# The start of an encoder layer on one core: dummy matmuls ahead of the data, and another cut and order of the first loads

## The chip, the cores and the metric

The kernel runs on one core of one Trainium2 chip. The metric is the device time of one execution in microseconds; the kernel before has a median of 1192.68 us over 3 runs (1192.55 to 1193.81). Engines are named as in the profile: PE is the matrix engine and PEld its weight loads, DVE the vector engine, ACT the scalar engine, POOL GpSimd, SP the engine that issues nearly all DMAs here.

## The reference

One encoder layer over 1024 tokens of width 1024, all in float32, cut to what matters here:

```python
hn = rms_norm(x, norm1_g)
proj = hn @ w_in                      # 2304 columns: qA | kA | vA | qB | kB | vB
out_a = global_gqa_attention(rope(norm(qa)), rope(norm(ka)), va)
out_b = dilated_mixture_attention(norm(qb), norm(kb), vb)
x = x + concat(rms_norm(out_a), rms_norm(out_b)) @ w_out
x = x + conv_ffn(rms_norm(x, norm2_g), w_up, conv_w, conv_b, w_down)
```

The change is confined to the loads and the first matmuls of `hn @ w_in`. The gain `norm1_g` is multiplied into the weights' rows, and the division by the root mean square of a token follows later, so the first matmuls need only `x`, `w_in` and `norm1_g`.

## The kernel before, in words

**Numbers.** A float32 operand is split into a high part, rounded by ACT (`split` L245, first line), and a low part, the difference, from DVE (L247). A product takes three matmuls: high by high, high by low, low by high. So every operand costs one ACT and one DVE instruction before PE can use all of it, and the first matmul of three needs ACT's half alone.

**Two kinds of work on PE at the start.** The 256 columns of kA and vA are projected plainly: for each of 8 token tiles, `kv_proj` (L294) does 8 contraction steps of 3 matmuls of 128x256, 24 in all, on L299, L300 and L301. Their weights `w_kv` are split by `kv_split` (L286), which also multiplies by the gain, and x by `x_prep` (L256), one split for each half (512 of the 1024 contraction rows) of a tile. The other 2048 columns are projected by a seven-product block scheme in two chunks; `in_unit` (L431) is one contraction step of one product over four token tiles, 12 matmuls of 128x512 on L437 to L439, with weights that `w_prep` (L402) makes from the blocks "11", "12", "21", "22" of `w_in`. The first product (4 units, 48 matmuls) takes x and block "11" alone; the second, n = 5, takes block "12" too, and sums of x halves (`x_sum` L262, `s_split` L279).

**Where x lies.** A tile's two halves are stored 4 tiles apart in one buffer: half h of tile tt at `qab((tt + 4h) % 8) + 512h` (L249). `x_load_t` (L252) loads both with one strided DMA of 512 KB.

**What sets the order.** A scheduler orders each engine's instructions within what the code's order and the buffers allow, and puts semaphore waits before them; engines then run their lists strictly in order. SP's DMAs take eight semaphores in turn (DMAHW0 to DMAHW7), so a DMA waits until the one eight before it on the list has landed. The start is L579 to L602: the two halves of `w_kv`, tile 0 of x, the gain vector (`norm1_g`, 32 bytes a partition), the other tiles 1 to 3, block "11", the splits, then the identity matrix, four small loads that spread the head gains over the partitions, x tiles 4 to 7, block "12", and the rows of x for the mean square (`n_load` L273, one buffer, read by `n_sq` L276 on ACT before the next load). `kv_tile` (L1186) does one tile: `kv_proj`, the `x_prep` of the tile two ahead, and `kv_out` (L309), in which ACT copies the tile's sums out of their PSUM bank (one of four) to a staging buffer at `F_UA + 256 * i`, whence a DMA stores them. `late_consts` (L616) and `bound` (L604) work on the head gains; `bound` uses scratch at `F_UA`, in the staging buffer of tile 0.

The whole program is emitted twice (`emit(True)`, `emit(False)`): the second copy runs only if the head gains are very large, which they are not here. After the first 250 or so matmuls the order of the instructions is not touched by the change.

Of the kernel before, what the change touches and what calls it, by code (L numbers as in the profile page):

```python
# [20 lines left out]
D = 1024  # L21
# [13 lines left out]
O_IDF = 0  # L35
O_GA = 128
O_GB = 384
# [19 lines left out]
SM_G1 = O_SM + 24  # L57
# [8 lines left out]
F_UA = O_F  # L66
F_W = [O_F + 2048 + 2048 * i for i in range(3)]
F_TMP = O_QAB + 512
F_KSQ = O_QAB + 768
F_NG = O_F + 9216  # L70
F_ROPE = O_F + 8192


# [60 lines left out]
C_12 = [O_QAB + 2048, O_QAB + 2560, O_F + 1536, O_F + 8704]  # L134

@with_exitstack
def tile_encoder_layer(ctx, tc, x, xT, w_in, w_kv, gains, norm1_g, norm2_g, w_out, w_up, convs,
                       w_down, ident, rope, tmx, tbc, cnt, tee, out):
    nc = tc.nc
    pool = ctx.enter_context(tc.tile_pool(name="arena", bufs=1))  # L140
    pspool = ctx.enter_context(tc.tile_pool(name="psum", bufs=1, space=bass.MemoryType.PSUM))
# [10 lines left out]
    def emit(bounded):  # L152

        act = nc.scalar.activation
        vec = nc.vector
        gp = nc.gpsimd
        mm = nc.tensor.matmul
        dma = nc.sync.dma_start

        def f(off, n):  # L160
            return bigf[:, off:off + n]

        def r(off, n):
# [33 lines left out]
        def perm_rows(t, b, width):  # L197
            rr, c = divmod(b, 2)
            return bass.AP(tensor=t.tensor, offset=t.offset + (512 * c + rr) * width, ap=[[4 * width, 128], [1, width]])

        def bcast(t, n, off=0):
            return bass.AP(tensor=t.tensor, offset=t.offset + off, ap=[[0, 128], [1, n]])
# [21 lines left out]
        def qab(tt):  # L224
            return O_QAB + 1024 * tt
# [16 lines left out]
        def a_op(n, t):  # L242
            return R_A[n] + 1024 * t

        def split(o, src):  # L245
            act(r(o, 512), src, AF.Copy)
            vec.tensor_tensor(r(o + 512, 512), src, rf(o, 512), op=OP.subtract)  # L247

        def x_at(tt, half):  # L249
            return qab((tt + 4 * half) % 8) + 512 * half  # L250

        def x_load_t(tt):  # L252
            a, b = [x_at(tt, half) for half in ((0, 1), (1, 0))[tt // 4]]
            dma(fp(a, [b - a, 2], [1, 512]), heads(xT[:, tt, :], 2))

        def x_prep(tt):  # L256
            for half in range(2):
                split(a_op(((1, 2), (3, 4))[tt // 4][half], tt % 4), f(x_at(tt, half), 512))

        x_raw = {5: lambda t: x_at(t + 4, 1), 7: lambda t: x_at(t + 4, 0), 6: lambda t: x_at(t, 0), 3: lambda t: x_at(t, 1)}  # L260
# [12 lines left out]
        def n_load(tt):  # L273
            dma(f(F_ROPE, 1024), perm_rows(x, tt, D))

        def n_sq(tt):  # L276
            act(f(F_ROPE, 1024), f(F_ROPE, 1024), AF.Square, accum_out=f(SM_SS1 + tt, 1))

# [1 line left out]
            split(a_op(n, t), f(x_raw[n](t), 512))  # L280


        def kv_load(half):
            dma(f(F_W[2] + 1024 * half, 1024), w_kv[half])

        def kv_split(k):  # L286
            o, raw, g = R_A[7] + 2048 * (k // 4) + 256 * (k % 4), f(F_W[2] + 256 * k, 256), f(SM_G1 + k, 1)
            act(r(o, 256), raw, AF.Copy, scale=g)
            vec.scalar_tensor_tensor(r(o + 1024, 256), raw, g, rf(o, 256), op0=OP.mult, op1=OP.subtract)
# [24 lines left out]
        def k4(o, j, n=64, off=0):  # L314
            return fp(o + 128 * j + off, [1024, 4], [64, 2], [1, n])
# [19 lines left out]
        def k_turn():  # L335
            for j in range(2):
                for o in (0, 16, 32, 48):
                    gp.tensor_tensor(k4(F_KSQ, j, 16, o), k4(F_TMP, j, 16, o ^ 16),
                                     fp(F_ROPE + 512 * j + 64 + o, [128, 4], [0, 2], [1, 16]), op=OP.mult)

        def k_add():
            for j in range(2):
                k = k4(F_TMP, j)
                vec.tensor_tensor(k, k, fp(F_ROPE + 512 * j, [128, 4], [0, 2], [1, 64]), op=OP.mult)
                vec.tensor_tensor(k, k, k4(F_KSQ, j), op=OP.add)
# [56 lines left out]
        def w_prep(m):  # L402
# [6 lines left out]
            if n == 5:  # L409
                act(b12, b12, AF.Copy, scale=g0)  # L410
                vec.scalar_tensor_tensor(b11, b11, f(F_NG + k, 1), b12, op0=OP.mult, op1=OP.add)
            if n == (6 if c else 3):
# [66 lines left out]
        def done(kind, t0, u, late=None):  # L479
# [5 lines left out]
            if kind == "kb":  # L485
                qo, qs = (O_QAB, 1024) if t0 else (F_ROPE, 256)
            elif late is not None:
# [88 lines left out]

            return square_at, mean_at, root_at, refine_at, norm_at, gain_at

        kv_load(0)  # L579
        x_load_t(0)  # L580
        dma(f(SM_G1, 8), norm1_g)
        kv_load(1)
        for i in range(1, 4):
            x_load_t(i)
        w_load(0, "11", 0, 2)
        w_load(0, "11", 2, 2)
        x_prep(0)
        for k in range(8):
            kv_split(k)
        x_prep(1)  # L590
        dma(f(O_IDF, 128), ident)
        for i, o in enumerate((O_GA, O_GA + 128, O_GB, O_GB + 64)):
            dma(f(o, 64), bcast(gains, 64, 64 * i))
        for i in range(4, 6):
            x_load_t(i)
        for i in range(6, 8):
            x_load_t(i)
        w_load(0, "12")
        n_load(0)
        w_load(0, "21", 0, 3)  # L600
        vec.tensor_copy(r(R_IDR, 128), f(O_IDF, 128))
        vec.tensor_scalar(f(F_NG, 8), f(SM_G1, 8), -1.0, None, op0=OP.mult)  # L602

        def bound():  # L604

            t = F_UA
            vec.tensor_tensor(fp(t, [64, 2], [1, 64]), fp(O_GA, [128, 2], [1, 64]), fp(O_GA, [128, 2], [1, 64]), op=OP.mult)
            vec.tensor_tensor(f(t + 128, 64), f(O_GB, 64), f(O_GB + 64, 64), op=OP.mult)
            vec.tensor_tensor(f(t + 128, 64), f(t + 128, 64), f(t + 128, 64), op=OP.mult)
            vec.tensor_reduce(f(t + 192, 3), heads(f(t, 192), 3), axis=AX.X, op=OP.max)  # L610
            vec.tensor_tensor(f(t + 192, 1), f(t + 192, 1), f(t + 193, 1), op=OP.mult)
            vec.tensor_tensor(f(t + 192, 1), f(t + 192, 1), f(t + 194, 1), op=OP.max)
            vec.tensor_scalar(f(O_LIM, 1), f(t + 192, 1), float(HD), None, op0=OP.mult)
            vec.tensor_scalar(f(O_LIM + 1, 1), f(O_LIM, 1), LIMIT, None, op0=OP.is_le)
# [639 lines left out]
        for m in range(4 * len(prods)):  # L1254
            c, n = prods[m // 4]
# [65 lines left out]
        for g in range(16):  # L1321
# [28 lines left out]
            if g > 3 and fills:  # L1350
                b, kv = grp(g - 2 if bounded else g - 1)
# [441 lines left out]
        for m in range(2, len(order)):  # L1793
            j, n = order[m]
# [10 lines left out]
            if n == 3 and j < NPAIR - 1:  # L1805
# [4 lines left out]
                b = [lambda j=j, t=t: taps(j, 0, (t,)) for t in range(1, 5)]  # L1810
# [17 lines left out]
        for m in range(len(steps)):  # L1828
            n, q = steps[m]
# [97 lines left out]
```

## Time and profile before

| | |
|---|---|
| median of 3 runs | 1192.68 us |
| the profiled execution | 1192.58 us |
| its span (first to last instruction) | 1190.8 us, so 1.8 us lie around it |
| PE busy | 1170.1 us, 98% |
| DVE, ACT busy | 1010.8 us (85%), 661.2 us (56%) |
| granted TensorE clock, mean | 0.999 |

Busy time of PE, 98%, includes the time in which its matmuls ran at half pace: the profile counts an instruction as busy as long as it takes. A row of the timeline has the start in us from the span's start, the duration, the engine, the source line, what is written and read, and in brackets how long the engine sat idle before and what ended that. Matmuls overlap: the distance between two starts is what one costs, the duration is longer.

### The profile page before, as it was taken

Reading aid. Unit: us, or ns where it says so; the run is one execution under the profiler, and the core shown is the slowest. Engines: PE = TensorE matmul, PEld = TensorE weight load, DVE = VectorE, ACT = ScalarE, POOL = GpSimd, SP = SyncE. Lnnn points to the kernel's source line nnn. Section 1 sums busy time; section 2 is a strip of 40 time slices with the busy share of each in tenths; the row PEclk is TensorE's granted clock in tenths of the full one; section 3 lists DMA queues with packets and bytes.
Section 4 is the critical chain, followed back from the end, with each engine's and each line's share of the span. In section 5 each row is a group of like instructions: output and inputs, shape, how many; then the busy total and the mean of one; then the engine's idle time right before and its main releaser. Section 6 shows DMA issues by size and latency. Waiting matters only on the chain.

```text
span 1190.8 us, 16352 instructions
## 1 busy us (share of the span) xinstructions
PE 1170.1 (98%) x5876; PEld 963.7 (81%) x5876; DVE 1010.8 (85%) x1430; ACT 661.2 (56%) x986; POOL 332.0 (28%) x236
## 2 busy tenths in 40 slices
PE   6999999999999999999999999999999999999998
PEld 5888887666679998887888888888888888888886
DVE  6887888899988788568999999999999997966663
ACT  6874747789897777336544353444435363543331
POOL 0000221510024420011456565655556414000000
PEclk9999999999999999999999999999999999999999
DMA  8555220020016555222223233332323257967862
GB/s 306 169 168 147 80 69 18 17 61 1 10 40 155 120 129 198 86 72 97 81 80 115 91 114 104 109 107 98 115 80 115 107 203 275 339 226 254 290 222 85
DMA packets 123286, 153.23 MB, mean 129 GB/s; under 512 B 51648, under 2 KB 79040, under 8 KB 123072
## 3 DMA queue, kind: packets, MB, share of 16 engines
q1 hardware_dynamic: 121056, 146.37, 38.1%
q0 software_dynamic: 2144, 5.77, 2.2%
q8 instruction: 47, 0.77, 0.3%
q14 instruction: 39, 0.32, 0.1%
HBM read 113.57 MB, written 33.82 MB: 124 GB/s over the span
## 4 chain that ended last, share of the span: by engine, by line
PE 88%; DVE 5%; DMA 2%; ACT 2%; POOL 1%; issue 1%; SPq 0%; ACTq 0%; DVEq 0%; POOLq 0%
PE ps L1562 12%; PE ps L1561 12%; PE ps L1560 12%; PE ps L740 6%; PE ps L1704 6%; PE ps L1702 6%; PE ps L1703 6%; PE ps L439 3%; PE ps L437 3%; PE ps L438 3%; PE ps L969 3%; PE ps L1004 2%; PE ps L1109 2%; PE ps L1111 2%; PE ps L1110 2%; PE ps L756 2%
## 5 line engine op out<-in xcount | busy, mean ns | idle before, releaser
L1560 PE MATMUL ps<-bigr 128*128 128x512 f32 x616 | 239.8, 390 | 0.5 <-ACT bigr L1163 0.5
L1561 PE MATMUL ps<-bigr 128*128 128x512 f32 x616 | 239.6, 389 | 0.0
L1562 PE MATMUL ps<-bigr 128*128 128x512 f32 x616 | 239.6, 389 | 0.0
L1599 DVE SCALAR_TENSOR_TENSOR bigf<-bigf 128x768 f32<-128x768 f32 (+1 forms) x176 | 193.4, 1135 | 0.7
L1528 ACT ACTIVATE bigr<-bigf 128x512 fp32r<-128x512 f32 x154 | 91.7, 622 | 141.6 <-POOL bigf L1520 109.0
L1682 ACT ACTIVATE bigr<-bigf 128x1024 fp32r<-128x1024 f32 (+1 forms) x99 | 83.9, 868 | 115.8 <-PE ps L1704 83.4
L1560 PEld LDWEIGHTS ps<-bigr 128*128 128x128 f32 x616 | 115.7, 188 | 25.0 <-ACT bigr L1163 0.9
L1562 PEld LDWEIGHTS ps<-bigr 128*128 128x128 f32 x616 | 115.7, 188 | 24.0
L1561 PEld LDWEIGHTS ps<-bigr 128*128 128x128 f32 x616 | 115.7, 188 | 23.8
L1683 DVE TENSOR_TENSOR bigr<-bigf,bigr 128x1024 fp32r<-128x1024 f32 (+1 forms) x99 | 97.5, 1007 | 26.4 <-ACT bigr L1682 21.6
L1702 PE MATMUL ps<-bigr 128*128 128x512 f32 x308 | 119.8, 389 | 0.0
L1703 PE MATMUL ps<-bigr 128*128 128x512 f32 x308 | 119.8, 389 | 0.0
L1704 PE MATMUL ps<-bigr 128*128 128x512 f32 x308 | 119.8, 389 | 0.0
L1529 DVE TENSOR_TENSOR bigr<-bigf,bigr 128x512 fp32r<-128x512 f32 x112 | 106.1, 950 | 3.0 <-ACT bigr L1528 2.6
L740 PE MATMUL ps<-bigr 128*66 128x512 f32 x384 | 99.8, 394 | 0.0
L437 PE MATMUL ps<-bigr 128*128 128x512 f32 x224 | 87.4, 390 | 0.0
L438 PE MATMUL ps<-bigr 128*128 128x512 f32 x224 | 87.2, 389 | 0.0
L439 PE MATMUL ps<-bigr 128*128 128x512 f32 x224 | 87.1, 389 | 0.0
L767 DVE TENSOR_TENSOR bigr<-bigf,bigr 128x1024 fp32r<-128x1024 f32 x64 | 81.0, 1271 | 5.3 <-ACT bigr L766 4.8
L1565 DVE TENSOR_TENSOR bigf<-ps,bigf 128x512 f32<-128x512 f32 x110 | 75.1, 682 | 5.1 <-PE ps L1562 4.8
L1529 POOL TENSOR_TENSOR bigr<-bigf,bigr 128x512 fp32r<-128x512 f32 x42 | 67.0, 1594 | 32.9 <-ACT bigr L1528 31.9
L740 PEld LDWEIGHTS ps<-bigr 128*66 128x66 f32 x384 | 50.9, 136 | 29.8
(220 smaller groups left out, 2380.8 us busy)
## 6 DMA issues: line engine op xcount, KB each, us to landing
bigf<-w_down SPq DMA_DIRECT2D x99, 256.0 KB, 4.0
bigf<-w_up SPq DMA_DIRECT2D x44, 512.0 KB, 3.5
bigf<-gscr SPq DMA_DIRECT2D x77, 256.0 KB, 4.1
gscr<-bigf SPq DMA_DIRECT2D x31, 512.0 KB, 2.7
bigf<-x SPq DMA_DIRECT2D x16, 512.0 KB, 4.4
bigf<-w_in SPq DMA_DIRECT2D x29, 256.0 KB, 3.1
bigf<-xT SPq DMA_DIRECT2D x8, 512.0 KB, 5.1
bigf<-w_out SPq DMA_DIRECT2D x8, 512.0 KB, 3.5
```

Source lines behind the costliest of these rows:

```text
L437: mm(o, r(a, 128), r(w, 512), start=(k == 0 and n != 2 and (c == 1 or n != 3)), stop=False, skip_group_check=True)
L438: mm(o, r(a, 128), r(w + 512, 512), start=False, stop=False, skip_group_check=True)
L439: mm(o, r(a + 512, 128), r(w, 512), start=False, stop=(k == 3), skip_group_check=True)
L740: mm(bank(ob)[0:66], r(w, 66), r(p + 512 * u, 512), start=(kt == 0 and i == 0), stop=(kt == 7 and i == 2))
L1529: low = lambda eng: eng.tensor_tensor(rp(o + 512, [128, 4], [1, 128]), src, rfp(o, [128, 4], [1, 128]), op=OP.subtract)
L1560: mm(bank(b), wh, th, start=(k == 0 and n in (1, 5, 6, 7)), stop=False, skip_group_check=True)
L1561: mm(bank(b), wh, tl, start=False, stop=False, skip_group_check=True)
L1562: mm(bank(b), wl, th, start=False, stop=(k == 3), skip_group_check=True)
L1599: vec.scalar_tensor_tensor(f(a + o, n), f(i + d, n), w_, f(a + o, n), op0=OP.mult, op1=OP.add)
L1702: mm(o, ah, r(d, 512), start=(q == 0 and n in (1, 5, 2)), stop=False, skip_group_check=True)
L1703: mm(o, ah, r(d + 1024, 512), start=False, stop=False, skip_group_check=True)
L1704: mm(o, al, r(d, 512), start=False, stop=(q == NQ - 1), skip_group_check=True)
```

## The change

- Ten matmuls of 128x128 on a buffer filled with ones (by POOL) stand ahead of everything on PE; their result in bank 7 is not used. The buffer is the one that `n_load` fills later.
- `norm1_g` is no array of its own any more: it stands in the 8 columns ahead of the `w_kv` weights, comes with the first quarter of them, and DVE copies it to its old place.
- `w_kv` comes in three DMAs (steps 0-1 with the gains, 2-3, 4-7), with the halves of x tile 0 in between as DMAs of their own; x tile 0's second split stands behind the first four weight splits.
- Every x tile is loaded by two DMAs of 256 KB, one for each half, and the array is laid out on the host so that no half has to be swapped. All eight tiles are issued ahead of the constants and block "12".
- The identity and the head gains, already spread over 128 partitions, are one array of 2 KB a partition with one DMA in place of five.
- `bound`'s scratch moves to `F_UA + 1024`, out of the staging buffer of the first four tiles.

```diff
+WARM = 10
         def x_load_t(tt):
-            a, b = [x_at(tt, half) for half in ((0, 1), (1, 0))[tt // 4]]
-            dma(fp(a, [b - a, 2], [1, 512]), heads(xT[:, tt, :], 2))
-
-        def x_prep(tt):
             for half in range(2):
+                dma(f(x_at(tt, half), 512), xT[:, tt, 512 * half:512 * half + 512])
+
+        def x_prep(tt, halves=(0, 1)):
+            for half in halves:
                 split(a_op(((1, 2), (3, 4))[tt // 4][half], tt % 4), f(x_at(tt, half), 512))
...
-        def kv_load(half):
-            dma(f(F_W[2] + 1024 * half, 1024), w_kv[half])
+        def kv_load(k, n):
+            o = 8 if k == 0 else 0
+            dma(f(F_W[2] + 256 * k - o, 256 * n + o), w_kv[:, 256 * k + 8 - o:256 * (k + n) + 8])
...
-        kv_load(0)
-        x_load_t(0)
-        dma(f(SM_G1, 8), norm1_g)
-        kv_load(1)
+        warm = f(F_ROPE, 256)
+        gp.memset(warm, 1.0)
+        for i in range(WARM):
+            mm(bank(7, 128), f(F_ROPE, 128), f(F_ROPE + 128, 128), start=True, stop=True)
+        kv_load(0, 2)
+        dma(f(x_at(0, 0), 512), xT[:, 0, 0:512])
+        kv_load(2, 2)
+        dma(f(x_at(0, 1), 512), xT[:, 0, 512:1024])
+        kv_load(4, 4)
         for i in range(1, 4):
             x_load_t(i)
         w_load(0, "11", 0, 2)
         w_load(0, "11", 2, 2)
-        x_prep(0)
-        for k in range(8):
+        vec.tensor_copy(f(SM_G1, 8), f(F_W[2] - 8, 8))
+        x_prep(0, (0,))
+        for k in range(4):
+            kv_split(k)
+        x_prep(0, (1,))
+        for k in range(4, 8):
             kv_split(k)
         x_prep(1)
-        dma(f(O_IDF, 128), ident)
-        for i, o in enumerate((O_GA, O_GA + 128, O_GB, O_GB + 64)):
-            dma(f(o, 64), bcast(gains, 64, 64 * i))
-        for i in range(4, 6):
+        for i in range(4, 8):
             x_load_t(i)
-        for i in range(6, 8):
-            x_load_t(i)
+        dma(f(O_IDF, 512), consts)
         w_load(0, "12")
         n_load(0)
...
-            t = F_UA
+            t = F_UA + 1024
```

The lists of SP differ from the first entry on. SP before, from the load of x tiles 1 to 3 on; w_in 128x1024 is half of block "11", 128x2048 is block "12", and a wait on DMAHWn is one for a landing:

```order
L254 DMA bigf<-xT 128x2x512 x3
L397 DMA bigf<-w_in 128x1024
L397 DMA bigf<-w_in 128x1024 [waits DMAHW0_49]
L591 DMA bigf<-ident 128x128 [waits DMAHW1_49]
L593 DMA bigf<-gains 128x64 [waits DMAHW2_49]
L593 DMA bigf<-gains 128x64 [waits DMAHW3_49]
L593 DMA bigf<-gains 128x64 [waits DMAHW4_49]
L593 DMA bigf<-gains 128x64 [waits DMAHW5_49]
L254 DMA bigf<-xT 128x2x512 [waits DMAHW6_49,DVE_49]
L397 DMA bigf<-w_in 128x2048 [waits DMAHW7_49]
L254 DMA bigf<-xT 128x2x512 [waits DMAHW6_49,DMAHW0_49]
L274 DMA bigf<-x 128x1024 [waits DMAHW1_49]
```

SP with the change, from block "11" on:

```order
L399 DMA bigf<-w_in 128x1024 [waits DMAHW3_49]
L399 DMA bigf<-w_in 128x1024 [waits DMAHW4_49]
L255 DMA bigf<-xT 128x512 [waits DMAHW5_49]
L255 DMA bigf<-xT 128x512 [waits DMAHW6_49]
L255 DMA bigf<-xT 128x512 [waits DMAHW7_49]
L255 DMA bigf<-xT 128x512 [waits DMAHW0_49]
L255 DMA bigf<-xT 128x512 [waits DMAHW1_49]
L255 DMA bigf<-xT 128x512 [waits DMAHW2_49]
L255 DMA bigf<-xT 128x512 [waits DMAHW3_49]
L255 DMA bigf<-xT 128x512 [waits DMAHW4_49]
L604 DMA bigf<-consts 128x512 [waits DMAHW5_49]
L399 DMA bigf<-w_in 128x2048 [waits DMAHW6_49,DVE_49]
```

Before, x tile 4 waits for DVE, and x tile 5 waits for tile 4's landing (DMAHW6) beside its own semaphore (DMAHW0); tiles 6 and 7 come further down, each behind the landing of the one before. With the change each half waits for nothing but its turn of the eight semaphores, and all of x stands ahead of the constants and block "12".

ACT's list begins differently. Before (L246 splits x tile 0, L288 splits `w_kv`):

```order
L246 ACT_TABLE_LOAD
L246 ACTIVATE bigr<-bigf 128x512 [waits DMAHW1_49]
L246 ACTIVATE bigr<-bigf 128x512
L288 ACTIVATE bigr<-bigf 128x256 [waits DMAHW2_49,DMAHW0_49]
L288 ACTIVATE bigr<-bigf 128x256 x3
L288 ACTIVATE bigr<-bigf 128x256 [waits DMAHW3_49]
```

With the change (L290 is `kv_split`, L247 the split of x):

```order
L290 ACT_TABLE_LOAD [waits DMAHW0_49]
L290 ACTIVATE bigr<-bigf 128x256 [waits DVE_49]
L247 ACTIVATE bigr<-bigf 128x512 [waits DMAHW1_49]
L290 ACTIVATE bigr<-bigf 128x256
L290 ACTIVATE bigr<-bigf 128x256 [waits DMAHW2_49]
L290 ACTIVATE bigr<-bigf 128x256
L247 ACTIVATE bigr<-bigf 128x512 [waits DMAHW3_49]
L290 ACTIVATE bigr<-bigf 128x256 [waits DMAHW4_49]
```

The load of ACT's function table stood ahead of every wait; now it stands behind the wait for the first quarter of `w_kv`.

Some 50 instructions further, ACT copies the last `kv_proj` tiles out of PSUM (L311 before, L313 with the change); L246 and L247 are splits of x sums, L277 and L278 are `n_sq`, and L413 and L415 scale quarters of block "22". Before:

```order
L311 ACTIVATE bigf<-ps 128x256 [waits DMAHW5_49,PE_49,Activation_49]
L246 ACTIVATE bigr<-bigf 128x512 [waits DVE_49]
L246 ACTIVATE bigr<-bigf 128x512 [waits PE_49]
L413 ACTIVATE bigf<-bigf 128x512 [waits DMAHW7_49]
L246 ACTIVATE bigr<-bigf 128x512 [waits DVE_49]
L311 ACTIVATE bigf<-ps 128x256 [waits DMAHW6_49,PE_49,Activation_49]
L277 ACTIVATE bigf<-bigf 128x1024 [waits DMAHW0_49]
```

With the change:

```order
L278 ACTIVATE bigf<-bigf 128x1024 [waits DMAHW0_49]
L313 ACTIVATE bigf<-ps 128x256 [waits DMAHW7_49,PE_49,Activation_49]
L247 ACTIVATE bigr<-bigf 128x512 [waits DVE_49] x2
L415 ACTIVATE bigf<-bigf 128x512 [waits DMAHW2_49]
L415 ACTIVATE bigf<-bigf 128x512 [waits DMAHW3_49]
L313 ACTIVATE bigf<-ps 128x256 [waits DMAHW1_49,PE_49,Activation_49]
```

Before, one quarter of block "22" stood between the last two copies out of PSUM; now two do, each with a landing to wait for.

More of the change, by code (lines that the diff above doesn't have):

```diff
@@ L136, in tile_encoder_layer @@
 @with_exitstack
-def tile_encoder_layer(ctx, tc, x, xT, w_in, w_kv, gains, norm1_g, norm2_g, w_out, w_up, convs,
-                       w_down, ident, rope, tmx, tbc, cnt, tee, out):
+def tile_encoder_layer(ctx, tc, x, xT, w_in, w_kv, consts, norm2_g, w_out, w_up, convs,
+                       w_down, rope, tmx, tbc, cnt, tee, out):
     nc = tc.nc
@@ L1907 @@
     arrays = {
-        "x": x, "xT": a(np.stack([np.roll(_lanes(x[r].T, D)[0], 512 * (t // 4), axis=-1) for t, r in enumerate(rows)], axis=1)),
+        "x": x, "xT": a(np.stack([_lanes(x[r].T, D)[0] for r in rows], axis=1)),
         "w_in": a(np.stack([np.stack([_lanes(w_in[:, at:at + 512], 512)[half] for half in range(2) for _, at in c])
                             for c in CHUNKS])),
-        "w_kv": a(_lanes(w_in[:, 512:768], 512)),
-        "gains": np.concatenate([a(qa_norm_g), a(ka_norm_g), a(qb_norm_g), a(kb_norm_g)]),
-        "norm1_g": a(a(norm1_g).reshape(8, 128).T), "norm2_g": a(norm2_g), "w_out": a(w_out), "w_up": a(w_up),
+        "w_kv": np.concatenate([a(norm1_g).reshape(8, 128).T, _lanes(w_in[:, 512:768], D)[0]], axis=1),
+        "consts": np.concatenate([ident] + [np.tile(a(g), (128, n)) for g, n in ((qa_norm_g, 2), (ka_norm_g, 2), (qb_norm_g, 1), (kb_norm_g, 1))], axis=1),
+        "norm2_g": a(norm2_g), "w_out": a(w_out), "w_up": a(w_up),
         "convs": a(np.concatenate([outg.reshape(8, 128), np.zeros((56, 128), np.float32), a(conv_w).reshape(132, 128),
@@ L1916 @@
         "w_down": a(w_down),
-        "ident": ident, "rope": rope, "tmx": tmx, "tbc": tbc, "cnt": cnt, "tee": tee,
+        "rope": rope, "tmx": tmx, "tbc": tbc, "cnt": cnt, "tee": tee,
     }
```

## The prediction

> **What bounds the kernel now.** I read the page's busy times first, then PE's timeline, then who ends the waits at the start.
>
> ```profile
> PE 1170.1 (98%) x5876; PEld 963.7 (81%) x5876; DVE 1010.8 (85%) x1430; ACT 661.2 (56%) x986; POOL 332.0 (28%) x236
> ```
>
> PE is the bound: what it need not wait for, and what it does faster, comes off the end. So the question is from which moment on it runs without a break. Its timeline at the places that I use:
>
> ```profile
> 7.66 0.58 PE L299 MATMUL ps<-bigr 128*128 128x256 f32 x1 [7.66 <-ACT bigr L288]
> ...
> 13.33 0.41 PE L301 MATMUL ps<-bigr 128*128 128x256 f32 x1
> 13.54 0.41 PE L299 MATMUL ps<-bigr 128*128 128x256 f32 x1
> ...
> 16.58 0.39 PE L437 MATMUL ps<-bigr 128*128 128x512 f32 x1
> ...
> 48.85 0.28 PE L301 MATMUL ps<-bigr 128*128 128x256 f32 x1
> 48.97 0.40 PE L437 MATMUL ps<-bigr 128*128 128x512 f32 x1
> 49.20 0.40 PE L438 MATMUL ps<-bigr 128*128 128x512 f32 x1
> ...
> 51.04 0.39 PE L437 MATMUL ps<-bigr 128*128 128x512 f32 x1
> ```
>
> The first matmul starts at 7.66. At 13.5 one of 128x256 follows the other after 0.21 us, at 48.9 after 0.12: PE ran at not much over half pace until then. At 16.58 the first two kA/vA tiles (48 matmuls) are done, at 48.97 all eight and the four units of the first product. Between the two, PE's groups by line (count, busy, mean ns, then idle time and its end):
>
> ```profile
> L301 PE MATMUL ps<-bigr 128*128 128x256 f32 x49 | 14.0, 285 | 0.2 <-DVE bigr L247 0.2
> L299 PE MATMUL ps<-bigr 128*128 128x256 f32 x48 | 13.9, 289 | 2.8 <-ACT bigr L246 2.8
> L300 PE MATMUL ps<-bigr 128*128 128x256 f32 x49 | 13.9, 283 | 0.0
> L438 PE MATMUL ps<-bigr 128*128 128x512 f32 x16 | 6.3, 391 | 0.0
> L437 PE MATMUL ps<-bigr 128*128 128x512 f32 x16 | 6.3, 391 | 0.0
> L439 PE MATMUL ps<-bigr 128*128 128x512 f32 x16 | 6.1, 392 | 0.0
> ```
>
> That is 144 of 128x256 (two more end the tile before) and 48 of 128x512, with 3.0 us of waits, 2.8 of them for splits of x. 48.97 is the mark: a us that it comes earlier is a us off the end, unless a new wait follows. The windows say how likely that is:
>
> ```profile
> 40.00:60.00 20.00, 20.00 (x126) 18.11 (x125) 18.84 (x32) 18.22 (x35) 0.00 (x0) 1.00 0.59 184
> 60.00:80.00 20.00, 20.00 (x90) 16.57 (x89) 16.87 (x36) 15.00 (x26) 0.00 (x0) 1.00 0.42 136
> ```
>
> After the window's 20.00 us stand PE, PEld, DVE, ACT, POOL. PE does not pause, but from 40 to 60 DVE and ACT have only 1.2 and 1.8 us to spare in 20; after that they have more. The gain can be lost there.
>
> **The first 48 matmuls.** What feeds them, from ACT's timeline and DVE's, the landing of the two `w_kv` loads from their line, and windows of 5 us whose last column is GB/s:
>
> ```profile
> 0.81 1.28 ACT L246 ACT_TABLE_LOAD   x1 [0.81 <-PEq L1919]
> ...
> 7.12 1.69 ACT L288 ACTIVATE bigr<-bigf 128x256 fp32r<-128x256 f32 x4
> 9.76 1.71 ACT L288 ACTIVATE bigr<-bigf 128x256 fp32r<-128x256 f32 x4 [0.95 <-DMA bigf<-w_kv]
> 11.38 1.14 ACT L246 ACTIVATE bigr<-bigf 128x512 fp32r<-128x512 f32 x2
> ```
>
> ```profile
> 12.03 1.29 DVE L247 TENSOR_TENSOR bigr<-bigf,bigr 128x512 fp32r<-128x512 f32 x2
> ```
>
> ```profile
> DMA to landing us min/median/max: 3.4/5.4/7.5
> ```
>
> ```profile
> 0.00:5.00 5.00, 0.00 (x0) 0.00 (x0) 0.00 (x0) 1.28 (x1) 0.20 (x4) 1.00 0.63 209
> 5.00:10.00 5.00, 2.11 (x8) 1.82 (x9) 2.97 (x7) 2.98 (x7) 0.00 (x0) 1.00 0.95 335
> 10.00:15.00 5.00, 5.00 (x29) 5.00 (x29) 3.48 (x7) 3.15 (x7) 0.00 (x0) 1.00 0.90 331
> ```
>
> The second `w_kv` load took 7.5 us and landed when ACT's wait ended, at 9.76; so it was issued at 2.26, and the first one, which is SP's first DMA, some 1.4 earlier, landed at about 4.2. A quarter of the weights should land at some 3.5. The table load now stands behind that landing: 3.5 + 1.28 = 4.8, plus one weight split (1.69 / 4 = 0.42) and half a tile's split (1.14 / 2 = 0.57): the first matmul at 5.8, 1.9 earlier. That is not the gain yet, for steps 4 to 7 need the second half of `w_kv`. Up to it 1.57 MB are asked for, as before, so 9.76 is one bound. The other: 1.05 MB by 5.0, the other 0.53 at 335 GB/s by 6.6, and as long until the landing is known as between 3.6 (0.52 MB, by the windows) and 4.2: 7.2. I take 8.7, nearer to the row; fewer bytes lie beside it and no gain vector in 32-byte rows. Then 1.71 for the splits and 1.14 for tile 1: ACT is done at 11.55, DVE 0.8 later (13.32 against 12.52 before) at 12.35. The last twelve matmuls of tile 1 need these, 12 x 0.12 = 1.4: it ends at 13.8, say 14.0, against 16.58. **First term 2.6 us**, from 1.4 (9.76) to 4.0 (7.2).
>
> The moved table load is hidden: by 4.8 + 1.69 + 1.14 = 7.6 ACT has caught up, before 8.7; uncovered, with the landing at 7.2, it costs 0.4. DVE's copy of the gains lies beside it.
>
> The ten dummies are float32; the nearest row is the float32 product of 128 columns in the attention stage:
>
> ```profile
> L1004 PEld LDWEIGHTS ps<-bigf x256: 135/138/143, 361.6 to 457.4; 128*65 128x65 f32 x128
> L1004 PE MATMUL ps<-bigf x256: 270/272/275, 361.7 to 457.5; 128*65 128x128 f32 x128
> ```
>
> ```profile
> 373.91 1.91 PE L1004 MATMUL ps<-bigf 128*65 128x128 f32 x16
> ```
>
> 128 matmuls leave 256 records, two each; sixteen records take 1.91 us, so one follows the other after (1.91 - 0.27) / 15 = 0.109. Twenty at the early pace (0.21 / 0.12 = 1.75 times as long) take 3.8 us: from about 1.3, half a us after ACT's first instruction, to 5.1. That is before the first real matmul at 5.8, so they cost nothing; laid end to end the rows give the upper bound, below. What they are worth is the pace: at 0.21 the 48 matmuls would take 10.1 us.
>
> **The next 192.** Their work is 144 x 0.12 + 48 x 0.23 = 28.3 us, and before they took 48.97 - 16.58 = 32.4. The difference, 4.1, is the waits of 3.0 and 1.1 lost where shapes alternate. Two causes of the waits, from ACT's timeline and the table of waits:
>
> ```profile
> 33.39 1.68 ACT L246 ACTIVATE bigr<-bigf 128x512 fp32r<-128x512 f32 x3 [0.89 <-DMA bigf<-xT]
> ```
>
> ```profile
> ACT bigf L277 <- DMA bigf<-x: 2.5, 3, 1.4
> ACT bigf L311 <- DVE bigf L613: 2.6, 1, 2.6
> ```
>
> L311 is ACT's copy into staging, held 2.6 us by `bound`'s scratch, with the splits of x queued behind it; and the last x tile came at 33.39. Both go. With the change x tile 2 is complete after 2.6 MB, block "11" after 4.2, tile 7 after 6.3; at 209, 335 and 331 GB/s that is 9.7, 14.4 and 20.8 us, with 2 us for the landing 11.7, 16.4 and 23. They are needed at 14.0 less 1.9 for the two engines' splits, at 19.8 (four tiles done), and after 30. Only tile 2 is tight; a us late costs a us. What comes later instead, the constants and block "12", is needed after 42. **Second term 4.1**, from 3.0 (the alternation still costs) to 4.1. The mark moves to 14.0 + 28.3 = 42.3.
>
> **A new wait.** PE's tenth matmul after the mark writes the bank that ACT's last copy empties, before at 49.56:
>
> ```profile
> 49.56 0.36 ACT L311 ACTIVATE bigf<-ps 128x256 f32<-128x256 f32 x1
> ```
>
> ```profile
> ACT bigf L413 <- DMA bigf<-w_in: 2.5, 3, 1.1
> ```
>
> It was done at 49.9 for a matmul at 51.04, 1.1 to spare. Now it stands behind one more scaling (L415; L413 takes 0.7 as L288's kind does) with a landing to wait for (up to 1.1, the row is from 60 to 190 us) and behind a Square that waits for rows of x (up to 1.4). At the worst 0.7 + 1.1 + 1.4 - 1.1 = 2.1; at the best nothing. **Third term -0.8**, nearer to the best since x comes ten us earlier for all of ACT's list.
>
> The sum: 2.6 + 4.1 - 0.8 = 5.9 off the profiled execution's 1192.58 (0.1 under the median; the 1.8 outside its span stay): **1186.7 us**. The other edits, the constants in one DMA among them, end no wait that PE sees.
>
> **The rivals.** What a measurement here can tell from no change is about 0.2%, 2.4 us.
>
> *The pace stays low* (20%). If matmuls of ones do not count, or the gaps between steps do, half pace lasts to 13.6 as before: 37 matmuls at 0.21 from 5.8, eleven at 0.12, 0.4 of waits: tile 1 ends at 15.3, 1.3 later, 1188.0. For it: here 5.9 us of matmuls (7.66 to 13.54) went by before the pace rose, longer than 3.8 of dummies. Against it: real ones follow within a us. [...]
>
> *ACT takes over* (12%). The third term is 3.0: DVE and ACT are 94% and 91% busy from 40 to 60 and cannot give back 6.7 us of lead. 2.6 + 4.1 - 3.0 = 3.7: 1188.9.
>
> *Small loads are slow* (4%). Halving x's loads leaves eight of 256 KB in flight. One load of half a MB at the start took as long as this, by the table of DMAs:
>
> ```profile
> bigf<-w_in SPq DMA_DIRECT2D x2, 512.0 KB, 11.2
> ```
>
> If 256 KB took that too, SP's eight turns would move 2.1 MB in 11.2 us, 187 GB/s. Block "12" (7.6 MB) then comes at 2 + 41 = 43, just in time; it decides below 167 GB/s, and at 150 PE goes on at 52.7 + 1.5 = 54.2 in place of 48.97, 5.2 later: 1197.8. Against it: 11.2 us were with 4 MB queued, and tile loads already came as two 2 KB rows a partition at 331 GB/s. [...]
>
> *The dummies are in the way* (4%). If each record's load and matmul lie end to end at half pace, (0.138 + 0.272) x 1.75 x 20 = 14.4, the dummies end at 15.7, and 48 x 0.12 + 28.3 lead to 49.8: 1193.4, no change. The pitch of 0.109 speaks against it.
>
> **The numbers.** My forecast has 58%, its own range 1185.0 to 1188.3; 2% are left for cases that I don't see. The range of 8 in 10 reaches up into the second rival, 1184.9 to 1189.2. Faster: 58 + 20 + 12 with a little of the rest, 0.91; same 0.05; slower 0.04.
>
> **What would show it.** On PE's timeline: dummies end before 5.8; tile 1 ends near 14.0; the first matmul of the second product stands at 42.3; pitch 0.12 from 12 us on. On ACT's: the table load at 3.5; no wait on DVE for L313. x tile 7 lands before 24. Third term: PE's wait at 44.4. I am wrong if the mark comes after 46, or if the mark is early and the end is not.

## The result, and the profile after

The changed kernel takes 1187.62 us (median of 6 runs, 1186.55 to 1188.86) against 1192.98 of the kernel before on the same chip: a ratio of 0.9955, 95% interval 0.9942 to 0.9967, so 5.4 us saved, with 3.9 to 6.9 as bounds. The forecast was 1186.7 in a range of 1184.9 to 1189.2. The profiled execution has a span of 1185.8 us, 5.0 under that of before. Medians and ratios, here and below, leave out two executions that ran far longer than all others: one of 1345.24 us (the fetch earlier) and one of 4172.92 us (half tiles, early table).

PE's timeline after the change, at the places that the prediction named:

```profile
1.18 4.64 PE L584 MATMUL ps<-bigf 128*128 128x128 f32 x20 [1.18 <-POOL bigf L582]
6.29 0.39 PE L301 MATMUL ps<-bigr 128*128 128x256 f32 x1 [0.47 <-ACT bigr L247]
...
8.99 0.39 PE L301 MATMUL ps<-bigr 128*128 128x256 f32 x1 [0.28 <-ACT bigr L290]
...
14.18 0.28 PE L301 MATMUL ps<-bigr 128*128 128x256 f32 x1
...
42.36 0.40 PE L439 MATMUL ps<-bigr 128*128 128x512 f32 x1
...
44.43 0.39 PE L439 MATMUL ps<-bigr 128*128 128x512 f32 x1
```

The dummies end at 5.82, the first real matmul starts at 6.29, and it already has the short duration: 0.39 us where the first one before had 0.58. The first 48 matmuls are done at 14.18 and the mark stands at 42.36, 6.61 us ahead of before. Between the two, PE's groups (count, busy, mean ns, idle time before) show no wait at all:

```profile
L303 PE MATMUL ps<-bigr 128*128 128x256 f32 x49 | 13.9, 283 | 0.0
L302 PE MATMUL ps<-bigr 128*128 128x256 f32 x49 | 13.9, 283 | 0.0
L301 PE MATMUL ps<-bigr 128*128 128x256 f32 x48 | 13.6, 283 | 0.0
```

The loads of x explain it: SP's issues (start, duration of all in the row) before, from tile 4 on (the third left out), and after.

```profile
13.89 0.38 SPq L254 DMA_DIRECT2D bigf<-xT  x1
18.30 0.38 SPq L254 DMA_DIRECT2D bigf<-xT  x1
...
28.27 0.38 SPq L254 DMA_DIRECT2D bigf<-xT  x1
```

```profile
3.17 3.69 SPq L255 DMA_DIRECT2D bigf<-xT  x6
9.71 6.26 SPq L255 DMA_DIRECT2D bigf<-xT  x8
```

Before, each of the last four tiles was issued when the one before had landed; now all eight halves are out by 16.

Of the 6.61 us not all arrive. The last matmul, before and after:

```profile
1185.36 0.39 PE L1704 MATMUL ps<-bigr 128*128 128x512 f32 x1
```

```profile
1179.57 0.39 PE L1711 MATMUL ps<-bigr 128*128 128x512 f32 x1
```

That is 5.79 ahead. The first place where PE waits after the mark is at 177, and ACT waits at 109 for a fetch (of the stored kA/vA tiles). Of each of the two, the row before, in which no wait stands, and the row after:

```profile
183.76 0.46 PE L192 MATMUL ps<-bigr 128*128 128x128 f32 x4
```

```profile
177.60 0.51 PE L193 MATMUL ps<-bigr 128*128 128x128 f32 x4 [0.29 <-DVE bigf L453]
```

```profile
115.06 0.62 ACT L324 ACTIVATE bigf<-bigf 128x512 f32<-128x512 f32 x1
```

```profile
109.38 0.63 ACT L326 ACTIVATE bigf<-bigf 128x512 f32<-128x512 f32 x1 [0.83 <-DMA bigf<-kvscr]
```

### The profile page after: what moved, and what is told of

The parts are those of the page before. It is cut to its first block, busy times and chain, and to the rows that moved or that the text cites. A ratio compares the mean times of both kernels' runs of the same rounds, so it can differ in the third digit from the quotient of the medians.

```text
span 1185.8 us, 16414 instructions
## 1 busy us (share of the span) xinstructions
PE 1172.6 (99%) x5896; PEld 966.2 (81%) x5896; DVE 1009.8 (85%) x1431; ACT 659.9 (56%) x986; POOL 332.1 (28%) x237
## 3 DMA queue, kind: packets, MB, share of 16 engines
q0 software_dynamic: 2144, 5.77, 2.2%
## 4 chain that ended last, share of the span: by engine, by line
PE 90%; DVE 5%; ACT 2%; POOL 1%; DMA 1%; issue 1%; SPq 0%; ACTq 0%; POOLq 0%; DVEq 0%
PE ps L1569 12%; PE ps L1568 12%; PE ps L1567 12%; PE ps L747 6%; PE ps L1709 6%; PE ps L1711 6%; PE ps L1710 6%; PE ps L439 3%; PE ps L440 3%; PE ps L441 3%; PE ps L976 3%; PE ps L1118 2%; PE ps L1116 2%; PE ps L1011 2%; PE ps L1117 2%; PE ps L763 2%
```

## The experiments

For each kernel the marks of its own profiled execution, read off PE's timeline: when the first 48 matmuls are done, the mark, the last matmul; then the time and its ratio to the kernel before, which ran beside each of them on the same chip (medians of 1192.56 to 1192.98 us).

| kernel | first 48 | mark | last matmul | time, us | ratio, 95% interval |
|---|---|---|---|---|---|
| before | 16.58 | 48.97 | 1185.36 | 1192.98 | |
| the change | 14.18 | 42.36 | 1179.57 | 1187.62 | 0.9955 (0.9942 to 0.9967) |
| the change again | 14.34 | 42.51 | 1179.97 | 1187.78 | 0.9961 (0.9949 to 0.9973) |
| change, no dummies | 15.75 | 43.93 | 1180.60 | 1187.27 | 0.9952 (0.9940 to 0.9965) |
| before + dummies | 16.73 | 48.17 | 1184.61 | 1193.12 | 1.0002 (0.9993 to 1.0010) |
| before + halves of x | 15.98 | 44.16 | 1181.06 | 1188.70 | 0.9963 (0.9950 to 0.9976) |
| change, strided x | 14.76 | 48.93 | 1185.62 | 1193.51 | 1.0007 (0.9996 to 1.0018) |
| change, scratch back | 14.76 | 42.94 | 1180.12 | 1187.03 | 0.9946 (0.9929 to 0.9962) |
| before + scratch moved | 15.83 | 48.84 | 1186.60 | 1192.78 | 0.9995 (0.9986 to 1.0005) |
| change, early table | 15.71 | 43.89 | 1180.75 | 1188.15 | 0.9957 (0.9941 to 0.9974) |
| change, half tiles | 14.18 | 42.36 | 1179.44 | 1187.73 | 0.9958 (0.9945 to 0.9970) |
| half tiles, early table | 15.73 | 44.13 | 1180.95 | 1187.51 | 0.9957 (0.9944 to 0.9970) |
| early table, fill | 15.26 | 43.44 | 1180.18 | 1188.16 | 0.9952 (0.9938 to 0.9966) |

The intervals are 1 to 2 us to either side, so a us between two kernels is told by the marks alone, and the marks are those of one execution each.

**The change again.** No edit.

> The changed kernel once more, as a yardstick for what two executions of one program differ by on PE's timeline. If the loss between the mark (the last matmul of the eight kA/vA tiles, at 42.36 us, 6.61 ahead of before) and the end (5.0 to 5.8 ahead) is part of the program, the marks repeat: last matmul of the tiles at 42.4 within 0.2, a first wait after it near 177 us of 0.2 to 0.4 us, the last matmul at 1179.6 within 0.2. If it is chance in one execution, the lead at the last matmul comes out anywhere between 5.3 and 6.6.

The mark repeats to 0.15, and so does the loss behind it: PE waits 0.54 at 178.04 (I had expected 0.2 to 0.4), and the lead goes from 6.46 to 5.39 (in the first execution from 6.61 to 5.79). The place belongs to the program; the size differs by 0.25 between two executions, and the last matmul by 0.4, more than I had allowed.

**No dummies.**

```diff
-WARM = 10
+WARM = 0
```

> The change without its ten dummies. My theory: the pace rises some 5.9 to 6.2 us after PE's first matmul, whatever it computes; without dummies that is at 12.3 in place of 7.4. The matmuls until then are held by landings anyway (second half of the weights at 8.4), so of the 48 only some 5 to 9 more than with dummies run at 0.21 in place of 0.12 on the path: the first 48 are done 0.5 to 1.0 later (14.7 to 15.2), the mark at 42.9 to 43.4, 1188.1 to 1188.6 us. Rival one, the dummies carry the whole first term of 2.6: mark at 44.9, 1190.2. Rival two, the pace follows from the real matmuls alone: no difference, mark at 42.4.

```profile
6.11 0.58 PE L301 MATMUL ps<-bigr 128*128 128x256 f32 x1 [6.11 <-ACT bigr L247]
...
13.20 0.33 PE L301 MATMUL ps<-bigr 128*128 128x256 f32 x1
13.37 0.28 PE L302 MATMUL ps<-bigr 128*128 128x256 f32 x1
```

PE's timeline without dummies: the pace (distance between two starts) was 0.21 until 13.2, passes there (0.17), and is 0.12 behind it. The first 48 end 1.57 later than with dummies and so does the mark: above my 0.5 to 1.0, below the 2.6 of the first rival, and no difference, the second rival, is not what this execution shows. Its size is one draw: when the pace comes differs by 1.7 us between two executions with the same instructions at the start (the last section). At the last matmul 1.0 is left of it (0.6 against the second execution). The time shows nothing: it is 0.4 us lower, well within the intervals.

**Dummies alone.**

```diff
+gp.memset(f(F_ROPE, 256), 1.0)
+for i in range(10):
+    mm(bank(7, 128), f(F_ROPE, 128), f(F_ROPE + 128, 128), start=True, stop=True)
 kv_load(0)
```

> The kernel before with the ten dummies and nothing else. My theory: the first 48 matmuls end 1.0 to 1.8 earlier (near 15.2 in place of 16.58), but PE's later waits for splits of x end when loads land (the last at 33.39, PE goes on at 34.07) and stay at their place, so the mark stays at 48.97 within 0.2 and the time is that of before, within 0.5 us. Rival: what the dummies gain is kept, mark at 47.2 to 48.0, 1191.2 to 1191.9 us.

```profile
1.18 4.63 PE L581 MATMUL ps<-bigf 128*128 128x128 f32 x20 [1.18 <-POOL bigf L579]
7.74 0.58 PE L299 MATMUL ps<-bigr 128*128 128x256 f32 x1 [1.93 <-ACT bigr L288]
...
14.05 0.34 PE L301 MATMUL ps<-bigr 128*128 128x256 f32 x1
...
33.28 0.39 PE L299 MATMUL ps<-bigr 128*128 128x256 f32 x1 [1.12 <-ACT bigr L246]
```

No time is gained, as my theory had it, but the reason is half another: the dummies buy no pace either. PE stands still for 1.93 us behind them, the first real matmul has the long duration again, and the pace comes at 14.0 as if there had been none. The mark is 0.8 earlier because the last x tile landed 0.8 earlier in this execution (PE goes on at 33.28, before at 34.07).

**The halves of x alone.**

```diff
-a, b = [x_at(tt, half) for half in ((0, 1), (1, 0))[tt // 4]]
-dma(fp(a, [b - a, 2], [1, 512]), heads(xT[:, tt, :], 2))
+for half in range(2):
+    dma(f(x_at(tt, half), 512), xT[:, tt, 512 * half:512 * half + 512])
```

> The kernel before with one part of the change: each x tile by two DMAs of 256 KB, one for each half, laid out on the host to match. Everything else stays: no dummies, the gains in five small loads, the scratch in the staging buffer. My theory: the strided load of both halves counted as a write to all that lies between them, so splits of tiles 2 and 3 waited for the loads of tiles 4 to 7, and these for one another; with exact halves the waits at 23.85, 28.95 and 34.07 go. The first 48 matmuls end at 16.6 as before, the next 192 take 28.3 to 29.5, the mark comes at 44.9 to 46.1, the time is 1188.8 to 1190.0. Rival: the 256 KB loads themselves or the scratch hold ACT as before, mark at 47 or later, 1191 or more.

From the first 48 (15.98) to the mark (44.16) it is 28.18 us, to the hundredth what the whole change takes, and PE's groups show no wait in it. 4.8 of the 6.6 us at the mark come from this edit, and the time, 1188.70, is what was expected. The rival is out: five small loads of constants and the scratch in the staging buffer are still there, ACT's copy is still held for 0.4 us by the scratch, and PE waits for none of it.

**The strided loads put back.** The same edit the other way round, in the changed kernel.

> The change with one part undone: x tiles 1 to 7 come by one strided DMA each again (both halves, as before), with the host layout to match; dummies, weights in three DMAs, one array of constants and the new scratch stay. My theory: the strided load is taken as a write to all between its two halves, so splits of tiles 2 and 3 wait for the loads of tiles 4 to 7 and these for one another; the order of PE goes back to 48 matmuls, 24 of the first product, and so on. The first 48 end at 14 to 15, then waits for landings come back, the last x tile lands at 33 to 38, the mark is at 48 to 52, the time 1192 to 1196: nearly all of the gain is lost, though every other part of the change is there. Rival: the exact halves are only a part, and dummies, weights and constants keep their 2.6 us and more, mark at 44 to 46.5, 1188.5 to 1190.5.

```profile
23.27 0.39 PE L301 MATMUL ps<-bigr 128*128 128x256 f32 x1 [1.19 <-ACT bigr L247]
...
29.50 0.39 PE L301 MATMUL ps<-bigr 128*128 128x256 f32 x1 [1.20 <-ACT bigr L247]
...
34.27 0.39 PE L301 MATMUL ps<-bigr 128*128 128x256 f32 x1 [0.44 <-ACT bigr L247]
...
48.93 0.40 PE L439 MATMUL ps<-bigr 128*128 128x512 f32 x1
```

```profile
13.40 0.38 SPq L255 DMA_DIRECT2D bigf<-xT  x1
...
28.47 0.38 SPq L255 DMA_DIRECT2D bigf<-xT  x1
```

Both traces are those of before again: four issues 4 to 6 us apart (first and last shown), three waits 5 to 6 us apart, the mark at 48.93 and the whole gain gone, although the first 48 end at 14.76 (the last starts at 14.64). Of the 1.8 us won until then PE loses 1.08 at once, waiting until 16.00 for the first split of block "11", since the first product follows again; the rest goes in the three waits. The instruction order says why these come back. In the kernel before, three splits on ACT, in this order, wait for these semaphores; beside each stands what it splits and which load's turn that semaphore is:

```
ACT split of tile 2, first half    waits DMAHW0, third turn: load of x tile 5
ACT split of tile 3, first half    waits DMAHW3, third turn: load of x tile 6
ACT split of tile 2, second half   waits DMAHW7, third turn: load of x tile 7
```

Half 0 of tile 5 lies at 1024 * 5, half 1 at 1024 + 512 (in columns of x's buffer), and the strided DMA counts as a write to all between, tile 2's first half (at 2048) included. So tile 2, landed at 12.5, and the first half of tile 3, landed at 13.8, waited for loads that landed at 23, 28 and 33. Tile 3's second half (at 7680) lies just outside the range of tile 7's load, and it did not wait for another tile: ACT splits it at 13.83, when its own load has landed.

**The scratch, both ways.** In the change `t = F_UA` in place of `F_UA + 1024`; in the kernel before the reverse.

> The change with the scratch of the bound on the gains back in the staging buffer of tile 0. In its order ACT's first copy into staging stands 18 places further down, behind the splits of all x tiles, so it holds nothing that PE needs before tile 4 of the kA/vA tiles at some 31 us. My theory, after the run with the halves alone: nothing is lost, mark at 42.4 within 0.2, time as with the change. Rival, the prediction as it stood: the hold of 2.6 us comes back to PE, mark at 44 to 45.

> The kernel before with the scratch moved out of the staging buffer and nothing else. My theory: ACT's copy is no longer held, PE's wait at 23.85 shrinks by up to 1.66, but the split that PE waits for at 34.07 waits for the last x tile, whose loads still follow one another; mark between 47.5 and 49.0, time of before within 1 us. Rival: the 2.6 us go to the end, mark at 46.4, 1190.2 us.

Back in the staging buffer it costs nothing: from 14.76 to 42.94 it is 28.18 once more (the mark is 0.5 later than the 42.4 that I expected within 0.2, because the second half of the weights came late and PE started it at 9.57, not 8.99). Moved alone, it gains nothing:

```profile
23.91 0.39 PE L299 MATMUL ps<-bigr 128*128 128x256 f32 x1 [2.45 <-ACT bigr L246]
```

The wait at 23.85 before did not shrink, it grew to 2.45, since PE arrived earlier and the landing of tile 5 ends it. The later waits do not show in this execution, because PE ran at half pace from 25.84 to 29.25; it comes at 34.06 to the kA/vA matmul for which it had waited until 34.07 before. That the 2.6 us by which ACT's copy was held were on PE's path is disproved both ways.

**The table load first.**

```diff
+gp.memset(f(SM_T, 1), 0.0)
+act(f(SM_T, 1), f(SM_T, 1), AF.Copy)
 kv_load(0, 2)
```

> The change with one more ACT instruction on one column at the very start, so that the load of the function table (1.28 us) does not wait for the first weights. My theory: the first real matmul moves from 6.3 to 5.8 or earlier, but tile 0's steps 4 to 7 wait for the second half of the weights (8.4) all the same, so the first 48 end at 14.2 within 0.3 and the mark stays at 42.4 within 0.3. Rival: the table load is on the path, mark 1.0 to 1.3 earlier, at 41.1 to 41.4.

```profile
8.15 0.28 PE L303 MATMUL ps<-bigr 128*128 128x256 f32 x1
9.56 0.45 PE L301 MATMUL ps<-bigr 128*128 128x256 f32 x1 [1.13 <-ACT bigr L290]
10.08 0.58 PE L302 MATMUL ps<-bigr 128*128 128x256 f32 x1
...
12.81 0.41 PE L302 MATMUL ps<-bigr 128*128 128x256 f32 x1
13.02 0.34 PE L303 MATMUL ps<-bigr 128*128 128x256 f32 x1
13.20 0.28 PE L301 MATMUL ps<-bigr 128*128 128x256 f32 x1
```

Theory and rival were both wrong: the mark comes 1.5 later. The first real matmul starts at 5.55, PE is through with its first twelve at 8.4, stands still for 1.13 us (the second half of the weights lands at 8.98, with the change at 8.40), and is back at half pace from 10 to 13.

**Two tiles by halves, without and with the early table.** x tile 1's first half is loaded ahead of the second half of the weights.

```diff
+kv_proj(0, range(4))
+kv_proj(1, range(4))
 def kv_tile(i):
-    kv_proj(i)
+    kv_proj(i, range(4, 8) if i < 2 else range(8))
```

> The change with the first two kA/vA tiles done by halves: steps 0 to 3 of tile 0, steps 0 to 3 of tile 1, then steps 4 to 7 of both, and x tile 1's first half loaded ahead of the second half of the weights, x tile 0's second half behind it. My theory: with the change PE has 12 matmuls to do until the second half of the weights lands (8.4 to 9.2), waits, and the first 48 end at 14.2 to 14.8; with 24 to do it does not wait, the first 48 end at 12.8 to 13.6 and the mark comes at 41.0 to 41.8. The end follows only as far as the other engines let it: the first wait after the mark, near 177 us, takes back all of the lead beyond some 5.6 to 6.0, so the last matmul stands at 1179.2 to 1180.0 as with the change, and the time is that of the change within 0.5. Rival: the lead is kept, last matmul at 1178.0 to 1178.8, time 1186.2.

```profile
10.92 0.39 PE L301 MATMUL ps<-bigr 128*128 128x256 f32 x1 [0.66 <-ACT bigr L247]
```

The wait did not go, it moved from 8.99 to 10.92: the second half of the weights lands at 8.6, ACT then has four weight splits and a split of x to do, and no order of PE's work changes that. The mark is the same to the hundredth, and my theory of it is wrong. The last matmul stands where I expected it, but not for my reason: nothing is lost near 177. Here the wait that the prediction's third term named comes. ACT's Square waits for rows of x, the last copy out of PSUM stands at 44.48 in place of 42.95, and PE's tenth matmul after the mark waits for it, which takes 0.6 of the lead of 6.61:

```profile
40.89 1.06 ACT L278 ACTIVATE bigf<-bigf 128x1024 f32<-128x1024 f32 x1 [1.44 <-DMA bigf<-x]
```

```profile
44.90 0.50 PE L439 MATMUL ps<-bigr 128*128 128x512 f32 x1 [0.31 <-ACT bigf L313]
```

> The two tiles by halves together with the early load of ACT's function table. With the early table alone PE finished its first 12 matmuls at 8.3, stood still until 9.56, lost its pace and had it again only at 13.0. My theory: with 24 matmuls at hand it does not stand still for over a us, so the pace holds: first real matmul at 5.5 to 5.9, no matmul after 8 at 0.21, first 48 done at 12.6 to 13.5, mark at 40.9 to 41.7. Rival: the weights' second half, behind one load more, lands so late (9.5 or later) that PE stands still all the same and loses the pace; first 48 at 14.5 or later, mark at 42.7 or later.

```profile
9.29 0.28 PE L303 MATMUL ps<-bigr 128*128 128x256 f32 x1
11.20 0.39 PE L301 MATMUL ps<-bigr 128*128 128x256 f32 x1 [1.63 <-ACT bigr L247]
```

```profile
6.00:12.83 6.83, 5.19 (x35) 4.24 (x34) 5.05 (x11) 5.25 (x12) 0.00 (x0) 1.00 1.02 374
12.83:16.24 3.41, 3.41 (x18) 3.41 (x18) 2.14 (x4) 1.57 (x4) 0.00 (x0) 0.50 1.03 395
16.24:20.00 3.76, 3.76 (x33) 3.76 (x33) 2.12 (x4) 2.92 (x7) 0.00 (x0) 1.00 1.09 400
```

The rival holds here: PE stands still for 1.63 us, and loses its pace, but only at 12.8, after it has worked for 1.6 us, and has it again at 16.2. The windows show it in the third number from the end, the granted clock: 1.00, then 0.50 for 3.41 us, then 1.00 again.

**The early table with a fill.** Five float32 matmuls of zeros between steps 3 and 4 of tile 0.

```diff
+if tt == 0 and k == 3:
+    for i in range(5):
+        mm(bank(0, 128), f(F_UA + 1280, 128), f(F_UA + 1280, 128), start=False, stop=False)
```

> The change with the early load of the function table, as before, and five float32 matmuls of 128x128 of zeros added onto tile 0's sums between its steps 3 and 4 (ten records, 1.1 us at the full pace), where PE stood still for 1.13 us in the run with the early table alone and lost its pace from 9.56 to 13.0. My theory, that standing still for over a us there is what lost the pace: now it holds. First real matmul at 5.5, the pitch of steps 4 to 7 and of tile 1 is 0.12 and not 0.21, the first 48 end at 13.8 to 14.9 (15.71 with the table alone), the mark at 42.0 to 43.1 (43.89 there). Rival: the pace falls on its own clock, whatever PE does in these 1.1 us; matmuls from 9.6 to 13 at 0.21 again, mark at 43.7 or later. In time the two differ by 1 us or less, which the measurement cannot tell.

```profile
6.36 0.58 PE L302 MATMUL ps<-bigr 128*128 128x256 f32 x1 [0.55 <-ACT bigr L248]
...
9.18 0.41 PE L304 MATMUL ps<-bigr 128*128 128x256 f32 x1
9.39 1.73 PE L307 MATMUL ps<-bigf 128*128 128x128 f32 x10
10.87 0.37 PE L302 MATMUL ps<-bigr 128*128 128x256 f32 x1
11.07 0.28 PE L303 MATMUL ps<-bigr 128*128 128x256 f32 x1
```

Inconclusive on its question. In this execution the dummies ended at 5.81, but brought no pace: the first twelve run at 0.21, so none could be lost, and the pace comes during the fill. It shows something else, that the dummies do not always work.

**The fetch earlier**, to find the loss behind the mark. The fetched tiles are overwritten by the staging of vB before they are used, so this kernel's k is another one; it serves for the order of the waits alone.

```diff
-for m, fn in ((28, k_fetch), ...
+for m, fn in ((24, k_fetch), ...
```

> The change with the fetch of the stored kA/vA tiles scheduled four units earlier, ahead of the last four stores of vB. With the change SP issues this fetch at 106.3 (4.95 us earlier than before, where PE is 6.61 ahead), ACT waits 0.8 us for its landing before it squares k, and that is the first place where the lead is lost; PE's own first wait follows near 177. My theory: with the fetch ahead of those stores ACT's wait for it is gone, PE's wait at 177 with it, and the lead at the last matmul is 6.2 to 6.6 in place of 5.4 to 5.8 (last matmul at 1178.8 to 1179.2). Rival: the stores of vB, which now stand behind the fetch, are late in its place, or the lead is lost elsewhere: the wait near 177 stays, last matmul at 1179.5 or later. The time itself cannot tell these apart (0.7 us).

```profile
104.90 2.56 ACT L478 ACTIVATE bigf<-bigf 128x512 f32<-128x512 f32 x4 [1.79 <-DMA bigf<-kvscr]
```

The rival holds: ACT waits for the same fetch one step earlier, 1.79 in place of 0.83, PE waits 1.2 at L193, the last matmul stands at 1182.72 and the time is 1189.22 (ratio 0.9972, 0.9961 to 0.9984). The last matmul is so late only in part because of the fetch: of the lead of 6.66 at the mark 4.68 is left behind the wait at 179, and another 1.6 goes from 558.7 to 562.2, where the granted clock was 0.50. That this path, fetch to ACT to DVE to PE, sets the wait near 177 fits, since delaying it by a us lengthened that wait by 0.9, and since in the run with half tiles, where the fetch landed in time, neither ACT at 109 nor PE near 177 waits; how to shorten it stays open.

## Why the prediction was right

*The first 48 matmuls*: 14.18 against 14.0 forecast, 2.4 against the term of 2.6. Its parts lie otherwise than in the working, and there was luck in the sum. By the marks, 0.6 come with the halves of x alone (15.98: the first matmul needs only half a tile, 6.72 in place of 7.66), 0.2 with the loads of weights and constants (15.75 without dummies), and 1.6 with the dummies. Each is a difference of single executions, and chance alone is larger than the two smaller ones: the kernel with the scratch moved has the same instructions at the start as the one before and ends its first 48 at 15.83 in place of 16.58, because its pace came 1.7 us earlier. The working let the weights' landing set the end; it does (the second half lands at 8.40, forecast 8.7), but only for a PE at full pace, and whether PE has it is partly chance.

*The next 192*: 28.18 against 28.3. The size was right, one cause was wrong. The step "Two causes of the waits" named the bound's scratch and the last x tile; the scratch is none, both runs on it say so, and ACT's wait of 2.6 on DVE was only the earlier of two things that PE's split waited for. The x loads are all of it. I had them as late, because each waited for the one before, and overlooked what the order of ACT before already showed: that tiles 2 and 3 waited for the loads of tiles 5 to 7. That the size came out all the same is because the change removes both named causes at once.

*A new wait*: forecast -0.8 at the mark, measured 0 there. ACT's last copy stands at 42.95 and PE passes 44.43 without a break; the rows of x and the quarters of block "22" that the copy stands behind had landed. But 0.82 and 1.07 are lost between the mark and the last matmul, half or more of it near 177 and just behind it. So the place was wrong, and that the size fits is luck: I looked for it where the engines have least to spare, and it came behind a fetch that was issued only 4.95 us earlier where PE was 6.61 ahead. The wait that I named does occur: with half tiles, at the same mark, it came and took 0.6, and in three other executions 0.15 to 0.3 (scratch back, early table, half tiles with it). The window that has DVE at its limit after the change (its busy time stands third, 20.00 of 20 us) shows PE at work throughout:

```profile
20.00:40.00 20.00, 20.00 (x126) 18.11 (x126) 20.00 (x46) 16.78 (x32) 0.00 (x0) 1.00 0.60 221
```

*The rivals.* "The pace stays low" did not happen in the profiled execution, and does in two others. The dummies lasted 4.64 us and not 3.8 (from record to record 0.21, twice the row's 0.109 and not 1.75 times), and of ten executions with dummies eight had the pace by 6.7 us. Those 4.64 us hold a whole stretch of 3.41, the beat that the traces show (last section), for one start in three, (4.64 - 3.41) / 3.41, by my estimate from these two numbers, which takes the place of the start in the beat as chance. In four of the ten the clock rose while the dummies ran (4.74 to 5.78), in four more after them or with their end (6.00 to 6.66). "ACT takes over" (3.0) was too large by two thirds. Small loads were not slow here: the 256 KB loads of x landed in a median of 6.6 us with up to eight under way, and PE waited for none. The dummies are not in the way: 4.64 us, not 14.4.

*The total* is 0.9 us above the forecast. Of the profiled execution's lead 5.79 are there at the last matmul and 5.77 when the last store of the output has landed (1183.19 against 1188.96), and 5.0 at the end of the span: 0.8 is lost in the program's closing semaphore waits and drains, which last 2.65 us in place of 1.83. Why is not known; 0.5 to 0.8 of it shows in all but one of the kernels here that end early.

## What to carry to other kernels

A strided DMA counted here as a write to all that it spans (put back into the change, it moved the mark from 42.36 to 48.93): look which landing ends an engine's wait, and whether that load's data is what the engine needs. Where several waits follow one another, removing an earlier one was worth nothing here while the last was tied to a landing: dummies and a freed scratch alone gave 0, the halves of x alone gave nearly three quarters by the marks (4.8 of 6.6 us) and some four fifths by the time. A lead won at the start was not paid out in full: of 6.61 us at the mark 5.79 were there at the last matmul, behind a fetch that was issued only 4.95 us earlier.

## What the runs showed of the hardware

The pace of PE did not come a fixed time after its first work. The kernels before and with the scratch moved run the same instructions until then (first matmul at 7.66 and 7.68), and the pace came at 13.8 in one and at 12.1 in the other:

```profile
11.85 0.41 PE L300 MATMUL ps<-bigr 128*128 128x256 f32 x1
12.06 0.34 PE L301 MATMUL ps<-bigr 128*128 128x256 f32 x1
12.25 0.28 PE L299 MATMUL ps<-bigr 128*128 128x256 f32 x1
```

The pace is the granted clock, and the traces record it. It stood at 0.50 or at 1.00, and in each of the fourteen executions all its switches lie whole multiples of 3.41 us apart. (Ahead of the first switch there is no record, and the windows print 1.00 although the matmuls run at half pace, 0.21 us from start to start.) In the 3.41 us ahead of each rise PE was busy for 86% or more; two stretches of 90% (halves of x alone) and 94% (no dummies) did not raise it.

It was lost as well: four times ahead of the last matmul in these executions, each time for 3.41 us. The stops of PE ahead of the four were 1.13 us (early table, lost at 9.73), 1.63 (half tiles with it, at 12.83), 2.45 (scratch moved, at 25.84) and 1.86 (the fetch earlier, at 558.74). But 21 other stops of 1.06 to 1.83 us kept the clock. This is the one of 1.83, in the change with strided x, which ends at 562.99:

```profile
560.00:567.00 7.00, 5.17 (x28) 4.05 (x27) 7.00 (x11) 3.61 (x7) 3.17 (x2) 1.00 0.00 0
```

So the length of a stop alone does not decide, and where it falls in the beat of 3.41 us is a cause that fits. The busy share of PE in the 3.41 us ahead does not settle it: it was 45 to 63% ahead of the four losses, and as low as 47% in stretches that kept the clock. What else counts stays open. The run made to settle the cause could not, since it had no pace to lose.
